# State-space mixer of a hybrid decoder block: y and z kept with channels in rows, norm factors applied at the output product

## The chip, the cores and the metric

The kernel runs on one core of a Trainium2 chip. The metric is the device time of one execution in microseconds; a kernel's time is the median over several runs. All tensors are float32. Where the kernel says "fp32r", a float32 value has been split into a high part and a low part, each held in a reduced form that TensorE takes at its quick rate, and a product is three products: high by high, high by low and low by high.

## The reference

One decoder block for a sequence of 1024 tokens and a width of 1024. A hidden state h feeds two token mixers, whose outputs are merged by gates; a gated conv-FFN follows. Only the first mixer, the state-space one (SSD), and what takes its output is touched here:

```
xbc = silu(causal_dwconv(xbc, conv_w, conv_b))
xs, bm, cm = split(xbc)                 # 16 heads of 64 channels; 2 groups, state 128
dt = softplus(dt_raw + dt_bias); a = -exp(a_log)
# in chunks of 128 tokens; l, s: tokens of a chunk
xd = xs * dt
a_cum = cumsum(dt * a)
decay = exp(where(s <= l, a_cum[l] - a_cum[s], -inf))
cb = einsum('bclgn,bcsgn->bclsg', cc, bc)
y_diag = einsum('bclsgr,bcsgrp->bclgrp', cb[..., None] * decay, xd)
states = einsum('bclgn,bclgrp->bcgrpn', bc, xd * decay_to_end)
prev = running state: prev * chunk_decay + states
y_off = einsum('bclgn,bcgrpn->bclgrp', cc, prev) * exp(a_cum)
y = y_diag + y_off + d_skip * xs
y = y * silu(z)
yg = y in 2 groups of 512 channels
yg = yg * rsqrt(mean(yg * yg) + 1e-5)
y_ssd = yg * norm_w
merged = gate_ssd * (y_ssd @ w_ssd_o) + gate_att * (y_att @ w_attn_o)
```

The norm's factor belongs to a token and a group of 512 channels, so that it can be applied to y, or to the two partial sums (channels 0 to 511, 512 to 1023) of the product with w_ssd_o.

## The kernel before

The kernel is one function with many nested helpers. The order of the instructions on TensorE (PE), VectorE (DVE), ScalarE (ACT) and the sync engine (SP) is fixed by the order in which the code calls them, so an instruction that waits holds back all that stands behind it on its engine. GpSimd (POOL) does a few elementwise steps. SP issues nearly every DMA, in the order of the code; a store that waits for its data holds back the loads behind it. In SBUF, 43 slots of 128 x 1024 float32 are handed out and taken back by name (SL.get, SL.put). In PSUM there are two buffers of two banks (ps_mm), two of one bank (ps_wa) and two single banks (ps_wb, ps_wc).

The stages that matter, in order of time:

*z.* z_mms (L979 to L986) makes z in seven products by four token blocks of 128, with h as the stationary operand and 512 columns of weights moving, so z has tokens in rows (partitions). z_out (L1005) applies silu and stores it to DRAM, one array of 128 tokens by 1024 channels for each chunk.

*The SSD loop* (L1285 to L1334) runs over 16 steps u, chunk c = u // 2 and group g = u % 2, and is filled with the products that make v (fill, which draws 3-product pieces from v_stream), so that TensorE has work while the others prepare. A step's work is spread over helpers:

- chunk_in, for the next step: four transposes bring x, which lies with channels in rows, to tokens in rows (px, in PSUM); ScalarE copies px to xtk; VectorE makes xd = xtk x dt, POOL makes xd times the decay to the end and y = xtk x d_skip; TensorE makes the product of B and C and the transpose of B, and VectorE puts the causal mask on the former.
- chunk_decay and chunk_mask, for the next step: ScalarE makes the decay between tokens, VectorE multiplies it with the masked product of B and C. The result Ms has a 128 x 128 matrix M for each of the group's 8 heads, with the source tokens s in rows.
- chunk_out: po, the product of C with the carried state (128 tokens by 512 channels, not for chunk 0), which VectorE scales by exp(a_cum) into tt; then eight products py with a head's M stationary and 64 columns of xd moving; VectorE adds py to y, POOL adds tt.
- chunk_state: the state that the chunk adds.
- chunk_norm, at every second step: puts a chain of small steps in a queue (later), from which the loop runs one to three at given places (run_bg): y times z on VectorE, squares summed over channels on ScalarE (free with tokens in rows, since the sum runs along the row), the factor, y times the factor on VectorE, the store of y.

The heart of chunk_out:

```
T.matmul(pq, CT[g][:, tok], po[:, g, :], start=True, stop=True)
V.tensor_tensor(v3(tt[:, gs]), v3(pq), bc64(ea[:, c, hs]), op=ALU.mult)
...
T.matmul(py[:, r * 64 : (r + 1) * 64], Ms[u % 3][:, r, :], xd[:, g * GW + r * 64 : g * GW + (r + 1) * 64], start=True, stop=True)
```

*Four blocks of q and k* (n = 0 to 3; w_q, w_k, w_q, w_k), each two halves of 24 products of 512 columns (block_half, which calls mm3). Between the halves stand rope for the block before (ScalarE copies it out of PSUM into qf, VectorE and POOL turn it, split makes a high part thhi on ScalarE and a low part thlo on VectorE), the split of the next block's weights (split_seq), turn_y and the stores of q or k (store_qk: 16 small stores, high and low part in turn). turn_y (L1351 to L1360) brings y, reloaded with tokens in rows by load_y (four arrays yr for 512 tokens at a time), to channels in rows by four transposes in PSUM, from which ScalarE and VectorE make the high and low part, times the norm's weight. Which pieces are turned behind which half is listed in turns.

*Eight blocks of w_ssd_o* (j = 0 to 7), each two halves of 24 products into the two banks of one ps_mm buffer; VectorE then multiplies both halves by one plus the tanh of the gate (mout, L1443) and SP stores them. Between the halves stand, on VectorE, the low part of the next block's weights and, for j = 1 to 4, four differences of w_down pieces that a later stage wants (down_sum, L890), whose loads (down_load) stand on SP behind the k stores.

Attention, the output product and the FFN follow and are not touched.

## Time and profile before

| | before |
|---|---|
| median of 3 runs | 1813.42 us |
| lowest and highest | 1812.23 and 1814.8 us |
| the profiled execution | 1813.67 us |
| its span on the core | 1811.8 us |
| mean granted TensorE clock | 0.999 |
| instructions | 23720 |
| data moved by DMA | 336.22 MB, 133385 packets |

The profile is of one execution, which took 1813.67 us in all, of which 1811.8 lie between its first and last instruction. "Busy" is the time in which an engine executes something; PE is TensorE's products and PEld its loading of stationary operands, which runs beside the products. The granted clock is the share of its full clock that the chip gave TensorE. In a timeline row stand the start in microseconds from the span's start, the duration, the engine, the line, the operation with its output and its inputs, the shapes, how many were put together in the row, and in brackets how long the engine had been idle and what ended that. A row of windows gives a stretch, its length, the busy time and number of instructions of PE, PEld, DVE, ACT and POOL, the granted clock, the share of DMA use and the GB/s. Since TensorE's products are pipelined, a product's duration in such a row is longer than the distance from its start to the next one's.

### The profile page before, as it was taken

Reading aid. Unit: us, or ns where it says so; the run is one execution under the profiler, and the core shown is the slowest. Engines: PE = TensorE matmul, PEld = TensorE weight load, DVE = VectorE, ACT = ScalarE, POOL = GpSimd, SP = SyncE. Lnnn points to the kernel's source line nnn. Section 1 sums busy time; section 2 is a strip of 40 time slices with the busy share of each in tenths; the row PEclk is TensorE's granted clock in tenths of the full one; section 3 lists DMA queues with packets and bytes.
Section 4 is the critical chain, followed back from the end, with each engine's and each line's share of the span. In section 5 each row is a group of like instructions: output and inputs, shape, how many; then the busy total and the mean of one; then the engine's idle time right before and its main releaser. Section 6 shows DMA issues by size and latency. Waiting matters only on the chain.

```text
span 1811.8 us, 23720 instructions
## 1 busy us (share of the span) xinstructions
PE 1788.3 (99%) x8587; PEld 1483.5 (82%) x8587; DVE 1300.5 (72%) x1973; ACT 908.7 (50%) x1758; POOL 148.2 (8%) x156
## 2 busy tenths in 40 slices
PE   7999999999999999999999999999999999999998
PEld 5788888877888888888888888888888888888887
DVE  7887885577664277777666876679898888876545
ACT  8554555665440155565566132655454554564532
POOL 0000000365220000000000103100000000000001
PEclk9999999999999999999999999999999999999999
DMA  9464337465579676656726979313232223378744
GB/s 377 187 204 151 106 105 274 168 209 190 195 187 356 202 198 167 179 153 161 222 77 216 359 248 379 117 55 121 93 133 105 94 101 113 117 240 299 254 153 157
DMA packets 133385, 336.22 MB, mean 186 GB/s; under 512 B 15234, under 2 KB 33554, under 8 KB 133268
## 3 DMA queue, kind: packets, MB, share of 16 engines
q1 hardware_dynamic: 130068, 324.21, 53.7%
q0 software_dynamic: 3200, 10.49, 1.5%
q8 instruction: 68, 1.11, 0.3%
q14 instruction: 49, 0.40, 0.1%
HBM read 239.41 MB, written 95.24 MB: 185 GB/s over the span
## 4 chain that ended last, share of the span: by engine, by line
PE 70%; DVE 4%; ACT 2%; issue 1%; DMA 1%; SPq 0%; POOL 0%; DVEq 0%; POOLq 0%; ACTq 0%
PE upx L1977 4%; PE upx L1978 4%; PE upx L1976 4%; PE o L1626 3%; PE dx L2365 2%; PE dx L2366 2%; PE dx L2364 2%; PE upy L1978 2%; PE upy L1976 2%; PE upy L1977 2%; PE dy L2365 2%; PE dy L2364 2%; PE dy L2366 2%; PE sc L1568 2%; PE ao L118 2%; PE mix L2052 2%
## 5 line engine op out<-in xcount | busy, mean ns | idle before, releaser
L1976 PE MATMUL upx<-t,wu_t 128*128 128x512 f32 x264 | 103.1, 391 | 0.5 <-DVE cv L2429 0.4
L1977 PE MATMUL upx<-t,wu_t 128*128 128x512 f32 x264 | 102.8, 390 | 0.2 <-DVE t L2107 0.2
L1978 PE MATMUL upx<-t,wu_t 128*128 128x512 f32 x264 | 102.8, 389 | 0.0
L1614 ACT COPY aT<-at 128x512 f32<-128x512 f32 (+2 forms) x96 | 46.1, 480 | 112.8 <-PE at L1613 112.8
L1950 ACT ACTIVATE wu_t<-sab 128x512 fp32r<-128x512 f32 x57 | 34.1, 627 | 128.1 <-DVE sab L1967 128.1
L95 DVE TENSOR_TENSOR g_lo<-gst,g_hi 128x1024 fp32r<-128x1024 f32 (+1 forms) x42 | 47.7, 1135 | 50.4 <-ACT g_hi L94 50.2
L1626 PE MATMUL o<-vt,aT 128*128 128x128 f32 x576 | 80.5, 276 | 0.0
L1626 PEld LDWEIGHTS o<-vt,aT 128*128 128x128 f32 x576 | 74.3, 191 | 2.2
L94 ACT ACTIVATE g_hi<-gst 128x1024 fp32r<-128x1024 f32 (+1 forms) x42 | 41.5, 989 | 66.1 <-DMA gst<-gld_s 36.2
L1587 DVE TENSOR_REDUCE nmx<-sc 128x1 f32<-128x640 f32 (+3 forms) x64 | 65.6, 1025 | 2.2
L1567 PE MATMUL sc<-kst,qst 128*128 128x512 f32 (+2 forms) x192 | 64.6, 344 | 0.6 <-ACT p L1589 0.5
L1568 PE MATMUL sc<-klo,qst 128*128 128x512 f32 (+2 forms) x192 | 62.9, 344 | 0.0
L1603 DVE RECIPROCAL rsm<-ssum 128x2 f32<-128x2 f32 x64 | 10.6, 166 | 70.0 <-ACT p L1600 40.0
L1994 DVE SCALAR_TENSOR_TENSOR ug<-cg,vec,ug 128x1023 f32<-128x1023 f32 (+1 forms) x44 | 56.3, 1280 | 6.1 <-ACT ug L1993 5.3
L1976 PEld LDWEIGHTS upx<-t,wu_t 128*128 128x128 f32 x264 | 49.6, 188 | 11.6 <-DVE cv L2429 1.3
L1954 DVE TENSOR_TENSOR wu_t<-sab,wu_t 128x512 fp32r<-128x512 f32 x57 | 39.3, 690 | 26.6 <-ACT wu_t L1950 26.6
L1977 PEld LDWEIGHTS upx<-t,wu_t 128*128 128x128 f32 x264 | 49.6, 188 | 10.7 <-DVE t L2107 0.5
L1978 PEld LDWEIGHTS upx<-t,wu_t 128*128 128x128 f32 x264 | 49.5, 188 | 10.3
L1994 DVE SCALAR_TENSOR_TENSOR uv<-cv,vec,uv 128x1023 f32<-128x1023 f32 (+1 forms) x44 | 56.2, 1277 | 0.9 <-ACT uv L1993 0.9
L2485 POOL TENSOR_TENSOR rsf<-rsf,nhalf 128x1 f32<-128x1 f32 x8 | 5.2, 655 | 623.5 <-DVE rsf L2484 623.5
L1605 DVE SCALAR_TENSOR_TENSOR p<-p,coef,p 128x128 f32<-128x128 f32 (+3 forms) x64 | 52.4, 819 | 2.3
L139 POOL TENSOR_TENSOR sqt<-sqt,nhalf 128x4 f32<-128x4 f32 x16 | 16.5, 1031 | 433.3 <-DVE sqt L138 433.3
(591 smaller groups left out, 5825.0 us busy)
## 6 DMA issues: line engine op xcount, KB each, us to landing
adas<-in_w_ada SPq DMA_DIRECT2D x32, 512.0 KB, 5.6
wuf<-in_w_up SPq DMA_DIRECT2D x22, 512.0 KB, 3.2
gld_s<-gsum SPq DMA_DIRECT2D x22, 512.0 KB, 2.8
gst<-gld_s SPq DMA_DIRECT2D x20, 512.0 KB, 4.5
wdt_raw<-wtd SPq DMA_DIRECT2D x20, 512.0 KB, 4.9
wuv<-in_w_up SPq DMA_DIRECT2D x19, 512.0 KB, 3.3
gld_a<-ug SPq DMA_DIRECT2D x33, 256.0 KB, 2.1
adat<-in_w_ada SPq DMA_DIRECT2D x16, 512.0 KB, 8.4
```

Source lines behind the costliest of these rows:

```text
L1567: T.matmul(sc[:, n0:n1], qs_[s][:, tsl], ks_[s][:, n0:n1], start=True, stop=False)
L1568: T.matmul(sc[:, n0:n1], qs_[s][:, tsl], kl[s][:, n0:n1], start=False, stop=True)
L1587: V.reduce_max(nmx[:, bq, s : s + 1], sc[:, :L], axis=AX.X, negate=True)
L1605: V.scalar_tensor_tensor(pr[0][:, :L], pr[1][:, :L], coef[:, bq : bq + 1], pr[0][:, :L], op0=ALU.mult, op1=ALU.add)
L1626: T.matmul(po_of[j, grp][:, qi, :], at[:, k, :], vt[j % 2][:, kt, :], start=(kt == 0), stop=(kt == i))
L1976: T.matmul(out_, wh, xh_, start=(k == 0 and first), stop=False, skip_group_check=not first)
L1977: T.matmul(out_, wh, xl_, start=False, stop=False, skip_group_check=not first)
L1978: T.matmul(out_, wl, xh_, start=False, stop=(k == end), skip_group_check=not first)
L1994: V.scalar_tensor_tensor(u[:, d:], c_[:, : S - d], fw[:, 2 - d : 3 - d], u[:, d:], op0=ALU.mult, op1=ALU.add)
L2364: T.matmul(o, gh[:, kk, tsl], wh, start=(k == 0 and not more), stop=False, skip_group_check=more)
L2365: T.matmul(o, gh[:, kk, tsl], wl, start=False, stop=False, skip_group_check=more)
L2366: T.matmul(o, gl[:, kk, tsl], wh, start=False, stop=(k == KF - 1), skip_group_check=more)
```

## The change

y and z are kept with channels in rows from the start.

- **z**: in z_mms weights are stationary and h moves, so that z comes out with channels in rows. It is stored in one array, a chunk's 128 tokens being 512 bytes in a row.
- **x**: the ScalarE copy xtk goes. VectorE makes xd from px in PSUM. POOL makes y = x times d_skip from the untransposed x, with d_skip as a column in vec (V_DS). The reload of x for the chunk after the next stands behind that.
- **y products**: xd is stationary now (64 columns, one head), M moves (128 columns). Two heads write to rows 0 to 63 and 64 to 127 of the same 128 columns, so 8 products fill the same bank.
- **Carried state**: four products with 128 columns of the state stationary and C moving, in place of one of 512 columns. exp(a_cum) must now run along the row: chunk_decay makes it with two exponentials of 64 rows each (eb) per step, from the rows of a_cum that are loaded for the decay anyway.
- **Norm**: channels lie across rows, so that the sum over them is made in two stages: VectorE adds up the squares of four 128-channel pieces (reduce_sum, into ssq), and TensorE adds over rows, one product per group with ssq stationary and one column of ones moving (norm_sums). These run in chunk_in two chunks later, for chunk 6 at step 14, and for chunk 7 ahead of the first w_q block. y is stored without its factor.
- **Factors**: behind the first half of the second block the 16 x 128 factors are turned by one transpose, stored (rsd), and reloaded as two rows that are spread over all partitions (rsr).
- **turn_y** becomes split_y, which makes the two parts from the reloaded y, with no transposes.
- **w_ssd_o**: a half block now goes to both banks of a ps_mm buffer, one for each group of channels (so_half); so_out multiplies each by its group's factors, adds them and applies the gate, four VectorE operations for a half block, where before it was one. The result goes into gth in place.

```diff
     def chunk_decay(u):
         c, g = divmod(u, 2)
+        if c > 0:
+            by_two = Ms[u % 3].rearrange("p (j two) t -> p two j t", two=2)
+            for n in range(2):
+                hp = slice(64 * n, 64 * n + 64)
+                A.activation(eb[hp, g], by_two[hp, n], AF.Exp)
...
-                T.matmul(o, xh_, wh, start=(k == 0 and first), stop=False, skip_group_check=not first)
-                T.matmul(o, xh_, wl, start=False, stop=False, skip_group_check=not first)
-                T.matmul(o, xl_, wh, start=False, stop=(k == KH - 1), skip_group_check=not first)
+                T.matmul(o, wh, xh_, start=(k == 0 and first), stop=False, skip_group_check=not first)
+                T.matmul(o, wh, xl_, start=False, stop=False, skip_group_check=not first)
+                T.matmul(o, wl, xh_, start=False, stop=(k == KH - 1), skip_group_check=not first)
...
-            SP.dma_start(zd[4 * half + q][:, c * HALF : (c + 1) * HALF], o)
+            SP.dma_start(zd[:, 4 * half : 4 * half + 4, 4 * c + q, :], o.rearrange("p (c t) -> p c t", t=P))
...
+        if c > 1 and g == 0:
+            norm_sums(pc[:, 2 * P : 2 * P + 2], c - 2)
...
-        A.copy(xtk[:, gs], px)
...
-        V.tensor_tensor(v3(xd[:, gs]), v3(xtk[:, gs]), bc64(dt[:, c, hs]), op=ALU.mult)
+        V.tensor_tensor(v3(xd[:, gs]), v3(px), bc64(dt[:, c, hs]), op=ALU.mult)
...
-        G.tensor_tensor(v3(y[:, gs]), v3(xtk[:, gs]), bc64(rows[:, R_DS + g * RH : R_DS + (g + 1) * RH]), op=ALU.mult)
+        G.tensor_tensor(p4(y[:, gs]), xch[c % 2][:, 4 * g : 4 * g + 4, :], vec[:, V_DS + 4 * g : V_DS + 4 * g + 4, None].broadcast_to([P, 4, P]), op=ALU.mult)
...
-            T.matmul(pq, CT[g][:, tok], po[:, g, :], start=True, stop=True)
-            V.tensor_tensor(v3(tt[:, gs]), v3(pq), bc64(ea[:, c, hs]), op=ALU.mult)
+            for j in range(4):
+                T.matmul(pq[:, j * P : (j + 1) * P], po[:, g, j * P : (j + 1) * P], CT[g][:, tok], start=True, stop=True)
+            V.tensor_tensor(p4(tt[:, gs]), p4(pq), eb[:, g], op=ALU.mult)
         py = ps_wb(f"py{c}_{g}")
         for r in range(RH):
-            T.matmul(py[:, r * 64 : (r + 1) * 64], Ms[u % 3][:, r, :], xd[:, g * GW + r * 64 : g * GW + (r + 1) * 64], start=True, stop=True)
+            T.matmul(py[64 * (r % 2) : 64 * (r % 2) + 64, r // 2 * P : r // 2 * P + P], xd[:, g * GW + r * 64 : g * GW + (r + 1) * 64], Ms[u % 3][:, r, :], start=True, stop=True, skip_group_check=True)
...
         def square():
...
+            SP.dma_start(yd[:, :, c * P : (c + 1) * P], y.rearrange("p (k t) -> p k t", t=P))
+            A.activation(zt, y, AF.Square)
+
+        def sums():
+            V.reduce_sum(ssq, zt.rearrange("p (g j t) -> p g t j", g=2, t=P), axis=AX.X)
             if c < 7:
                 load_z(c + 1)
...
+    def norm_sums(ps, c):
+        need(("y", c))
+        for g in range(2):
+            T.matmul(ps[:, g : g + 1], ssq[:, g, :], ones[:, :1], start=True, stop=True)
+        V.tensor_copy(ssy[:, :, c], ps)
...
-            SP.dma_start(yr[q], yd[4 * half + q])
+            SP.dma_start(yr[q], yd[:, 2 * q : 2 * q + 2, half * HALF : (half + 1) * HALF])
...
+            if u == 14:
+                norm_sums(ps_wc("norms6")[:, :2], 6)
...
-        for q in range(4):
-            T.transpose(ps[:, q * P : (q + 1) * P], yr[q][:, k * P : (k + 1) * P], ident)
...
+    def split_y(k, half):
+        t = yT[k][half] = new_hl(f"yT{k}_{half}")
+        nw, src = vec[:, V_SN + k : V_SN + k + 1], yr[k // 2][:, k % 2, :]
+        A.activation(t[:, 0, :], src, AF.Copy, scale=nw)
+        V.scalar_tensor_tensor(t[:, 1, :], src, nw, t[:, 0, :].bitcast(F32), op0=ALU.mult, op1=ALU.subtract)
...
+        pn = ps_wc("norms")
+        norm_sums(pn[:, :2], 7)
+        SL.put(sm2)
+        for g in range(2):
+            rstd_of(ssy[:, g], ssy[:, g], 1.0 / GW, 1e-5)
         for n in range(4):
...
                 if n == 1 and half == 0:
                     load_y(1)
+                    pn = ps_wb("normT")
+                    T.transpose(pn[:16, :P], ssy.rearrange("p g c -> p (g c)"), ident)
+                    V.tensor_copy(f(dtc)[:16, :], pn[:16, :P])
+                    SP.dma_start(rsd, f(dtc)[:16, :])
...
+        rsr = [SL.get(f"rsr{g}") for g in range(2)]
+        for g in range(2):
+            SP.dma_start(rsr[g], rsd[8 * g : 8 * g + 8].rearrange("c t -> (c t)")[None].broadcast_to([P, S]))
+
+        def so_half(j, half):
+            ps = ps_mm(f"so{j}_{half}")
+            for g in range(2):
+                mm3(ps[:, g, :], [((seq_w[j + 4][0][:, k, :], seq_w[j + 4][1][:, k, :]), (yT[k][half][:, 0, :], yT[k][half][:, 1, :])) for k in range(4 * g, 4 * g + 4)])
+            return ps
+
+        def so_out(ps, gth, half):
+            hsl = slice(half * HALF, (half + 1) * HALF)
+            for g in range(2):
+                V.tensor_tensor(sev[:, g, :], ps[:, g, :], rsr[g][:, hsl], op=ALU.mult)
+            V.tensor_tensor(sev[:, 0, :], sev[:, 0, :], sev[:, 1, :], op=ALU.add)
+            V.scalar_tensor_tensor(gth[:, hsl], gth[:, hsl], 1.0, sev[:, 0, :], op0=ALU.add, op1=ALU.mult)
...
-            block_half(ps[:, 1, :], seq_w[j + 4], yT, 1)
-            for half in range(2):
-                hsl = slice(half * HALF, (half + 1) * HALF)
-                V.scalar_tensor_tensor(mout[:, hsl], gth[:, hsl], 1.0, ps[:, half, :], op0=ALU.add, op1=ALU.mult)
+            so_out(ps, gth, 0)
+            so_out(so_half(j, 1), gth, 1)
```

Three places show how the order of the engines moves; in each, the first block is the order before and the second the order with the change, with the line, the operation, output and inputs, and the shape.

TensorE at the end of the SSD loop: py is the last y product, v_7 the last piece of the v products that fill the loop, and w_qp the first block of w_q.

```order
L1221 MATMUL py_1_3919<-xd,M_2452 128x64 x8
L1152 MATMUL v_7_3892<-wv_3_hi,hT_1_264 128x512
L1153 MATMUL v_7_3892<-wv_3_lo,hT_1_264 128x512
L1154 MATMUL v_7_3892<-wv_3_hi,hT_1_264 128x512
L1152 MATMUL v_7_3892<-wv_3_hi,hT_1_266 128x512
L1153 MATMUL v_7_3892<-wv_3_lo,hT_1_266 128x512
L1154 MATMUL v_7_3892<-wv_3_hi,hT_1_266 128x512
L116 MATMUL w_qp_3967<-hT_0_78,w_q_hi 128x512
L117 MATMUL w_qp_3967<-hT_0_78,w_q_hi 128x512
```

```order
L1227 MATMUL po_1_3947<-xbcT_2177,prev_2694 128x128 x4
L1231 MATMUL py_1_3953<-M_2438,xd 64x128 x8
L1160 MATMUL v_7_3922<-wv_3_hi,hT_1_264 128x512
L1161 MATMUL v_7_3922<-wv_3_lo,hT_1_264 128x512
L1162 MATMUL v_7_3922<-wv_3_hi,hT_1_264 128x512
L1160 MATMUL v_7_3922<-wv_3_hi,hT_1_266 128x512
L1161 MATMUL v_7_3922<-wv_3_lo,hT_1_266 128x512
L1162 MATMUL v_7_3922<-wv_3_hi,hT_1_266 128x512
L1275 MATMUL norms<-ones,sm_1136 128x1 x2
L117 MATMUL w_qp_4005<-hT_0_78,w_q_hi 128x512
```

The y products come in another shape, the product with the carried state in four pieces, and two one-column sums (norms) stand between the last v product and the first product of w_q; they read what the norm's chain makes of the last chunk (sm holds ssq).

The sync engine, from the last store of v to the first stores of q: yd is y in DRAM, yr its reload, thhi and thlo the parts of the turned q, rsd the factors.

```order
L1168 DMA vd_597<-vev 128x512
L1255 DMA yd_605<-yt_2704 128x1024
L1271 DMA yr_3667<-yd_602 128x1024
L1271 DMA yr_3668<-yd_603 128x1024
L1271 DMA yr_3669<-yd_604 128x1024
L1271 DMA yr_3670<-yd_605 128x1024
L455 DMA qd_653<-thhi 16x1024
L456 DMA qd_653<-thlo 16x1024
```

```order
L1176 DMA vd_591<-vev 128x512
L1255 DMA yd<-yt_2690 1024x1x128
L1280 DMA yr_3687<-yd 128x2x512
L1280 DMA yr_3688<-yd 128x2x512
L1280 DMA yr_3689<-yd 128x2x512
L1280 DMA yr_3690<-yd 128x2x512
L1417 DMA rsd<-dtc 16x128
L457 DMA qd_640<-thhi 16x1024
L458 DMA qd_640<-thlo 16x1024
```

The reload stands where it stood, in another shape and from the one array; the store of the factors is new, between the reload and the first store of q.

VectorE in the first two w_ssd_o blocks: so is the product in PSUM, mout or gth what is stored, wdr the w_down pieces, w_ssd_o_lo the low part of the next block's weights.

```order
L95 TENSOR_TENSOR w_ssd_o_lo<-w_ssd_o_raw,w_ssd_o_hi 128x1024
L1443 SCALAR_TENSOR_TENSOR mout_4391<-gth_4389,so_4397 128x512 x2
L95 TENSOR_TENSOR w_ssd_o_lo<-w_ssd_o_raw,w_ssd_o_hi 128x1024
L890 TENSOR_TENSOR wdr_4445<-wdr_4445 128x512
L890 TENSOR_TENSOR wdr_4445<-wdr_4446,wdr_4445 128x512
L890 TENSOR_TENSOR wdr_4446<-wdr_4446,wdr_4445 128x512
L890 TENSOR_TENSOR wdr_4446<-wdr_4446 128x512
L1443 SCALAR_TENSOR_TENSOR mout_4392<-gth_4390,so_4487 128x512 x2
```

```order
L1435 TENSOR_TENSOR sev<-so_1_4426,rsr_4351 128x512
L1435 TENSOR_TENSOR sev<-so_1_4426,rsr_4352 128x512
L1436 TENSOR_TENSOR sev<-sev 128x512
L1437 SCALAR_TENSOR_TENSOR gth_4355<-gth_4355,sev 128x512
L96 TENSOR_TENSOR w_ssd_o_lo<-w_ssd_o_raw,w_ssd_o_hi 128x1024
L891 TENSOR_TENSOR wdr_4410<-wdr_4410 128x512
L891 TENSOR_TENSOR wdr_4410<-wdr_4411,wdr_4410 128x512
L891 TENSOR_TENSOR wdr_4411<-wdr_4411,wdr_4410 128x512
L891 TENSOR_TENSOR wdr_4411<-wdr_4411 128x512
L1435 TENSOR_TENSOR sev<-so_0_4459,rsr_4351 128x512
L1435 TENSOR_TENSOR sev<-so_0_4459,rsr_4352 128x512
```

The second block begins with the second half of block 0, the row before it (not shown) being the same four operations for its first half. Each half block is now emptied by four operations, where before one row of two emptied both; the first half of block 1 is emptied behind the four differences, ahead of its second half.

85 lines of the change are left out of this document (34 added, 51 removed).

## The prediction

> **What bounds the kernel now.** I read the busy line of the page first, then the chain of waits, then a table by stretches for the stages that the change touches, then the waits of TensorE's weight loads.
>
> ```profile
> PE 1788.3 (99%) x8587; PEld 1483.5 (82%) x8587; DVE 1300.5 (72%) x1973; ACT 908.7 (50%) x1758; POOL 148.2 (8%) x156
> ...
> PE 70%; DVE 4%; ACT 2%; issue 1%; DMA 1%; SPq 0%; POOL 0%; DVEq 0%; POOLq 0%; ACTq 0%
> ...
> 325.00:490.00 165.00, 164.67 (x864) 132.00 (x863) 113.44 (x159) 95.30 (x244) 78.62 (x64) 1.00 0.56 196
> 490.00:575.00 85.00, 84.92 (x402) 70.54 (x401) 50.65 (x61) 24.10 (x30) 13.64 (x4) 1.00 0.75 229
> ...
> PEld so L118 <- DVE w_ssd_o_lo L95: 0.5, 1, 0.5
> ```
>
> TensorE has work in 164.67 of 165 us of the SSD stage and in 84.92 of 85 us behind it; the only wait near the w_ssd_o blocks is one of 0.5 us. So each microsecond of TensorE's own work that goes in these stages shortens the program, and each new wait of TensorE lengthens it. VectorE (113 of 165 us) and ScalarE (95) set nothing as long as they stay just ahead. That is the whole question here: the change takes matmul time away and puts dependences in its place.
>
> **What TensorE saves.** Three bursts of the timeline price it.
>
> ```profile
> 489.58 1.47 PE L1357 MATMUL ytr<-ident,yr 128*128 128x128 f32 x12
> ...
> 491.12 0.40 PE L117 MATMUL w_kp<-hT,w_k_hi 128*128 128x512 f32 x1
> ...
> 360.01 1.02 PE L1217 MATMUL po<-prev,xbcT 128*128 128x512 f32 x2
> 360.87 1.89 PE L1221 MATMUL py<-xd,M 128*128 128x64 f32 x16
> ...
> 362.88 0.39 PE L1153 MATMUL v<-wv_lo,b 128*128 128x512 f32 x1
> ...
> 78.23 0.39 PE L118 MATMUL gs<-hT,wgs_lo 128*128 128x512 f32 x1
> 78.55 3.64 PE L745 MATMUL dt<-hr,dtw 128*32 128x512 f32 x32
> ...
> 82.46 0.40 PE L117 MATMUL gs<-hT,wgs_hi 128*128 128x512 f32 x1
> ```
>
> Starts matter here, not durations: in a steady block a 512-column product starts every 0.23 us (476.63 to 477.79 in a later fence, five of them). The row behind a burst is the second product of the next block, so the burst ended 0.23 us ahead of it.
>
> *The y transposes.* Twelve take 491.12 - 0.23 - 489.58 = 1.31 us, 0.109 each. All 64 go: **-7.0 us**.
>
> *The y products.* One burst (8 heads, 16 passes) takes 362.88 - 0.23 - 360.87 = 1.78 us, 0.11 per pass, though it moves only 64 columns: the load of 128 stationary columns sets the pace. Now 64 columns are stationary and 128 move. A float32 pass of 512 columns takes (360.87 - 360.01)/2 = 0.43, so one of 128 takes 0.107 to 0.11. Whether two heads run side by side shows in the dt product, which already writes four column groups: 32 passes of 0.43 would take 13.8 one by one; it takes from 78.46 (78.23 + 0.23) to 82.23, 3.77 us. That is 8 times 0.43 and 0.33 for getting into the grouped layout and out of it. So a new burst costs 8 x 0.11 + 0.33 = 1.21, saving 0.57; sixteen save **-9.1 us**. Bounds: no overlap, 16 x 0.11 + 0.33 = 2.09, +5.0 in all; no cost of changing layout, 0.88, -14.4. I take the dt row, which is the same mechanism with four groups for two.
>
> The Trainium skill ("TensorE: Matmul & The Clock Gate", Part 3) gives 2.38 times for three column groups, not three. By that share two groups would run 1.6 times as fast, a burst would take 1.44, the saving would be 5.5 us, and the sum below would be 1819.7. The dt row of this trace, 4.0 times for four groups, disagrees, and the trace decides.
>
> **What TensorE gains.** The carried-state product is cut in four 128-column pieces: 8 passes of 0.11 for two of 0.43, +0.04 in 14 places, **+0.5 us**. The sums over channels add 16 one-column products: 32 passes, each held by the load of 128 columns at 0.11, +3.5, and about 0.3 for the transpose of the factors and for two sums that stand alone: **+3.8 us** (between 1 if a one-column pass needs no full load and 4.5). The z products and the w_ssd_o products keep number and size; only what is stationary or where a sum is split changes: 0.
>
> So TensorE's own work falls by 11.8 us. ScalarE loses the copies of x and gains two exponentials per step, VectorE loses the scaling and gains one reduction per chunk; both have a third of the stage idle, so I cost that at nothing (28 exponentials of about 0.63, as the 512-wide ScalarE row below, are 18 us and eight reductions of 1.2 are 10 us if that cover is gone). More and smaller packets for z and y lie under 0.56 of DMA use; nothing waits for them within two steps.
>
> **New wait 1: the last chunk's norm sum.** It stands in TensorE's queue between the last v product and the first w_q block, and needs y of chunk 7 finished, times z, squared and summed.
>
> ```profile
> 476.63 0.39 PE L1153 MATMUL v<-wv_lo,hT 128*128 128x512 f32 x1
> ...
> 477.79 0.39 PE L116 MATMUL w_qp<-hT,w_q_hi 128*128 128x512 f32 x1
> ...
> 476.54 0.69 DVE L1223 TENSOR_TENSOR yt<-py,yt 128x512 f32<-128x512 f32 x1 [1.03 <-PE py L1221]
> 477.38 1.29 POOL L1227 TENSOR_TENSOR yt<-yt,tt 128x512 f32<-128x512 f32 x1 [6.12 <-DVE yt L1223]
> 478.70 1.23 DVE L1259 TENSOR_TENSOR yt<-yt,zt 128x1024 f32<-128x1024 f32 x1 [1.47 <-POOL yt L1227]
> 480.01 0.63 ACT L1247 ACTIVATE zt<-yt 128x512 f32<-128x512 f32 x1 [1.44 <-DVE yt L1259]
> ...
> L1587 DVE TENSOR_REDUCE nmx<-sc 128x1 f32<-128x1024 f32 x16 | 19.6, 1225 | 0.5
> ```
>
> Today nothing on TensorE waits for this chain, and w_q starts at 477.79. In the changed order the square starts at 480.01, takes 1.06 (a 1024-wide ScalarE row, below), the reduction 1.23 and two handovers 0.15: 482.45. Leaving the grouped layout puts TensorE 0.15 later, at 477.94. Wait: **+4.5 us**. Behind it stand the whole w_q block and all that follows. The sums of the other chunks are asked for a full step later and cost nothing.
>
> **New wait 2: the store queue behind rope.** SP's order is what changed. The reload of y (second half) and the store of the turned factors stand ahead of the 16 q stores. The reload now waits for the y splits of ScalarE and VectorE, no longer for TensorE's transposes; the factor store waits for a VectorE copy behind those splits.
>
> ```profile
> 477.99 0.59 ACT L1167 COPY vev<-v 128x512 f32<-128x512 f32 x1 [4.33 <-PE v L1154]
> ...
> 491.94 1.03 ACT L1378 ACTIVATE qf<-w_qp 128x1024 f32<-128x1024 f32 x1
> 499.13 1.06 ACT L94 ACTIVATE thhi<-qf 128x1024 fp32r<-128x1024 f32 x1 [6.16 <-DVE qf L1382]
> ...
> 501.36 1.22 DVE L95 TENSOR_TENSOR w_q_lo<-w_q_raw,w_q_hi 128x1024 fp32r<-128x1024 f32 x1
> 502.50 2.06 DVE L1360 SCALAR_TENSOR_TENSOR yT<-ytr,vec,yT 128x512 fp32r<-128x512 f32 x3
> ...
> 497.56 1.75 SPq L1271 DMA_DIRECT2D yr<-yd  x4
> 500.21 0.32 SPq L455 DMA_DIRECT2D qd<-thhi  x1
> ...
> 508.57 0.42 SPq L456 DMA_DIRECT2D qd<-thlo  x1
> 509.03 0.42 SPq L455 DMA_DIRECT2D qd<-thhi  x1
> ...
> 511.11 1.06 ACT L94 ACTIVATE thhi<-qf 128x1024 fp32r<-128x1024 f32 x1 [6.70 <-DMA qd<-thhi]
> ```
>
> I count from the end of the first w_q block, 489.58 today. ScalarE can take the result 0.2 later (477.79 to 477.99); today it comes to it at 491.94. From its start the rope and low-part chain takes 12.6 to the end of the third y split (504.56). So the copy is done at 13.0 and the q stores start at 13.4, where today they start at 10.6 and would now be ready at 8.5. They follow each other by 0.46; the last store of the high part is issued at 13.4 + 14 x 0.46 = 19.9, and the next rope may overwrite it 2.1 later (509.03 to 511.11), at 22.0. Behind that rewrite on ScalarE and VectorE stand the parts of the second w_k block: high part at 24.0, low part (two VectorE operations of 1.2) at 25.5. Without transposes the block is due at 22.0 (two blocks of 48 products, 10.9 each, and one turn). It can start at about 25.0: **+3.0 us**.
>
> What is late next: four y splits stand ahead of each following rope on ScalarE, 2.4 us. The third rope starts at 26.4, and its chain of 10.6 (491.94 to 502.58) with 0.6 of VectorE's own splits brings the first w_ssd_o low part at 37.6; the block, due at 36.0, needs it with its third product: **+1.2 us**. The fourth rope starts at 38.5, the next low part is done at 49.8.
>
> **New wait 3: fewer banks.** A half block now fills a pair of banks, so a bank must be emptied within one half block, 5.5 us, where today it had a block. Each half takes four VectorE operations for one.
>
> ```profile
> 539.98 1.28 DVE L1443 SCALAR_TENSOR_TENSOR mout<-gth,so 128x512 f32<-128x512 f32 x2
> ...
> 537.69 0.32 SPq L458 DMA_DIRECT2D khd<-thhi  x1
> ...
> 546.70 1.79 SPq L885 DMA_DIRECT2D wdr<-in_w_down  x4
> ...
> 553.75 0.69 DVE L890 TENSOR_TENSOR wdr<-wdr 128x512 f32<-128x512 f32 x1
> ```
>
> In VectorE's order the first emptying stands behind that low part: 49.8 + 1.28 = 51.1, block 1 is due at 48.1: +3.0, where today 0.5 is lost: **+2.5 us**. The emptying of block 1 stands behind the four w_down differences, whose loads stand behind the k stores: 9.0 from the first store to the loads and 7.7 to the last difference. Stores from 47.5 put it at 64.2, the bank free at 65.5; block 2 is due at 62.0: 3.5, or 2.6 if the stores pack better; I take **+3.0 us**. From block 3 on I find a microsecond or more to spare, with four operations, 2.7 us of VectorE, per 5.5.
>
> **The sum**, on the profiled execution (1811.8 span, 1813.67 in all, 0.25 above the median of 1813.42): -7.0 - 9.1 + 0.5 + 3.8 + 4.5 + 3.0 + 1.2 + 2.5 + 3.0 = +2.4, so **1816 us**: the saving is spent on waits.
>
> **The rivals.** *The clock falls in wait 1 (slower).* TensorE stands idle for 4.5 us, longer than anywhere in today's program behind the first microseconds.
>
> ```profile
> 14.85 1.22 PE L257 MATMUL xbc<-hT,wf_hi 128*128 128x512 f32 x2 [1.94 <-ACT hT L227]
> ...
> 19.29 1.05 PE L257 MATMUL gs<-hT,wf_hi 128*128 128x512 f32 x2
> 20.14 1.16 PE L216 MATMUL xbc<-hr,ones 128*128 128x512 f32 x2
> ...
> 1805.12 0.39 PE L2366 MATMUL dx<-wdt_hi,g_lo 128*128 128x512 f32 x1
> ...
> 1805.00:1811.00 6.00, 0.51 (x3) 0.08 (x1) 2.32 (x5) 0.69 (x2) 0.54 (x1) 0.83 0.47 175
> ```
>
> After the last matmul the granted clock averages 0.83 over 6 us: half speed for the last 2, so it fell some 3.7 us after it. At the start two products took 0.85 (19.29 to 20.14), half speed, 5.3 us after dense work began. 5.3 us at half speed lose 2.6: 1818.7. It decides where the wait passes the point at which the clock falls, which is near 4.5. The Trainium skill (same page, Part 1) has a free-running window of 3.4 us, which would hit an idle 4.5 one time in three and need at least 3.4 us to release; the trace's 3.7 agrees, with one case.
>
> *Store and bank waits are shorter (not slower).* If the q stores are out by 10.6 as today, wait 2 goes (4.2 us), and the fourth rope starts a microsecond earlier: about 5.5 less, 1810.5. For it: each step rests on a margin of about a microsecond. Against: the order on SP is fixed.
>
> *No overlap of column groups* (the change doesn't do what it says): 14.1 more, 1830. Against it stands the dt row.
>
> *VectorE falls behind in the w_ssd_o blocks or the SSD loop*: one further wait like the 3.0 in two or three blocks, 1823; VectorE's 50.65 of 85 us plus some 33 for the emptying is close (16 halves, three more operations of 0.69 each).
>
> **Chances.** Forecast 0.45 (own range 1812 to 1820), clock 0.18, shorter waits 0.19, no overlap 0.07, VectorE 0.11. Range 1805 to 1828: the low end is the shorter waits with the layout change free, the high end short of no overlap. 0.2%, about what a measurement can tell, is 3.6 us: slower (above 1817) 0.48, all of clock, VectorE and no overlap and 0.12 of the forecast; within 0.38, which is 0.28 of the forecast and 0.10 of the shorter waits; faster (below 1810) the remaining 0.14.
>
> **What would show it.** y products that start in pairs 0.01 apart, a burst of 1.2; TensorE idle about 4.5 before the first w_q block, released by the reduction; q stores starting behind the factor store; idle of some 3, 1, 3 and 3 us before the second w_k block and the first three w_ssd_o blocks. Wrong would be bursts near 2 us, or blocks that follow each other without gaps.

## The result, and the profile after

The changed kernel takes 1828.51 us (median of 4 runs, 1827.87 to 1828.95), the kernel before 1813.88 in the same comparison (4 runs): a ratio of 1.0081, with a 95% interval of 1.0064 to 1.0099. It is slower, by about 14.6 us. Forecast were 1816 with a range of 1805 to 1828: the sign was that of the forecast, the size was not, and the time lies half a microsecond outside the range.

The profiled execution spans 1826.5 us, 14.7 more than before. The page's busy line and the chain of waits of the changed kernel:

```profile
PE 1786.0 (98%) x8640; PEld 1478.9 (81%) x8640; DVE 1323.9 (72%) x2016; ACT 917.0 (50%) x1745; POOL 143.3 (8%) x150
...
PE 84%; DVE 7%; ACT 3%; DMA 2%; issue 2%; POOL 1%; SPq 1%; DVEq 0%; POOLq 0%; ACTq 0%
```

TensorE is busy 2.3 us less, in a span 14.7 us longer. Where it stands idle from the SSD loop to the w_ssd_o blocks is in the list of its waits (line, releaser, microseconds in total, times, the longest):

```profile
PE norms L1275 <- DVE sm L1259: 6.4, 2, 5.0
PE so L117 <- DVE sev L1435: 5.8, 2, 4.1
PE w_kp L117 <- ACT w_k_hi L95: 3.8, 1, 3.8
PE px L1275 <- DVE sm L1259: 1.0, 1, 1.0
PE v L1161 <- DVE wv_lo L932: 0.5, 1, 0.5
PE w_kp L119 <- DVE w_k_lo L96: 0.2, 1, 0.2
```

That is 17.7 us, where TensorE of the kernel before is without work for 0.4 (0.33 and 0.08) by the two windows that the prediction shows of these stages. The waits are longer than the whole loss, so other terms of both signs must stand beside them. The timeline has the four long waits at these rows:

```profile
482.20 0.98 PE L1275 MATMUL norms<-ones,sm 128*128 128x1 f32 x4 [5.00 <-DVE sm L1259]
...
522.16 0.79 PE L117 MATMUL w_kp<-hT,w_k_hi 128*128 128x512 f32 x1 [3.83 <-ACT w_k_hi L95]
...
549.24 0.47 PE L117 MATMUL so<-yT,w_ssd_o_hi 128*128 128x512 f32 x1 [1.67 <-DVE sev L1435]
...
564.48 0.76 PE L117 MATMUL so<-yT,w_ssd_o_hi 128*128 128x512 f32 x1 [4.08 <-DVE sev L1435]
```

and a table of windows, laid where the clock record changes, shows what follows them (stretch, length, busy time and number of instructions of PE, PEld, DVE, ACT, POOL, then the granted clock, the DMA share and GB/s):

```profile
477.50:480.91 3.41, 0.00 (x0) 0.00 (x0) 1.97 (x2) 2.25 (x3) 0.28 (x1) 1.00 0.93 320
480.91:487.74 6.83, 5.54 (x15) 4.61 (x16) 5.63 (x10) 1.33 (x2) 4.08 (x2) 0.50 0.31 84
518.46:521.87 3.41, 0.00 (x0) 0.00 (x0) 0.68 (x1) 1.76 (x2) 0.00 (x0) 1.00 0.77 211
521.87:528.70 6.83, 6.31 (x14) 4.57 (x15) 6.80 (x9) 3.60 (x6) 1.17 (x1) 0.50 0.68 122
559.42:562.83 3.41, 0.98 (x5) 0.48 (x3) 2.41 (x4) 0.00 (x0) 0.00 (x0) 1.00 0.96 273
562.83:569.66 6.83, 5.18 (x12) 4.13 (x13) 6.51 (x10) 1.06 (x1) 0.00 (x0) 0.50 0.82 291
```

In each of the waits of 5.0, 3.8 and 4.1 us the granted clock falls to 0.50 and stays there for 6.83 us. TensorE is busy for 5.54, 6.31 and 5.18 us of these stretches. Products of 512 columns start 0.427 apart there (484.04, 484.47, 484.89 in the timeline) and 0.227 apart at full clock, so that 47% of that busy time is lost: 2.6, 3.0 and 2.4, together 8.0 us. (The expectations below reckon with half of the time from the end of each wait: 2.8, 3.3 and 2.6, together 8.6. That is 0.6 too much.)

The balance is drawn from the first v product to the first product of attention, 292.1 us before (323.89 to 616.00) and 307.8 after (324.47 to 632.29): 15.7 more. The waits behind the loop make 14.8 of it (5.0, 3.8 and 0.2, 1.7, 4.1), half clock 8.0, the small waits in the loop 2.8 (1.0 and 0.5, and the other 1.4 of norms) less the 0.4 of before. What is left, -9.5, is put down to TensorE's own work, forecast at -11.8; it is a difference and was not measured as such, and experiment 8 finds about 2 us more of hold-ups in the loop that this list does not show. The stages behind, which the change does not touch, happen to be 1.4 us shorter in this profile than in that of the kernel before (1187.7 from 632.29 to the last product at 1819.95, for 1189.1 from 616.00 to 1805.12), and what lies ahead of the loop is 0.6 longer: together about the 14.7 of the spans.

### The profile page after: what moved, and what is told of

Same layout as the page of the kernel before. It is cut to its first block, busy times and chain, and to the rows that moved or that the text cites. A ratio compares the mean times of both kernels' runs of the same rounds, so it can differ in the third digit from the quotient of the medians.

```text
span 1826.5 us, 23848 instructions
## 1 busy us (share of the span) xinstructions
PE 1786.0 (98%) x8640; PEld 1478.9 (81%) x8640; DVE 1323.9 (72%) x2016; ACT 917.0 (50%) x1745; POOL 143.3 (8%) x150
## 4 chain that ended last, share of the span: by engine, by line
PE 84%; DVE 7%; ACT 3%; DMA 2%; issue 2%; POOL 1%; SPq 1%; DVEq 0%; POOLq 0%; ACTq 0%
PE upx L2001 4%; PE upx L2000 4%; PE upx L2002 4%; PE o L1650 3%; PE dx L2388 2%; PE dx L2390 2%; PE dx L2389 2%; PE upy L2001 2%; PE upy L2000 2%; PE upy L2002 2%; PE sc L1592 2%; PE dy L2388 2%; PE dy L2390 2%; PE dy L2389 2%; PE sc L1591 2%
## 5 line engine op out<-in xcount | busy, mean ns | idle before, releaser
L1627 DVE RECIPROCAL rsm<-ssum 128x2 f32<-128x2 f32 x64 | 10.6, 166 | 70.1 <-ACT p L1624 40.0
L2000 PEld LDWEIGHTS upx<-t,wu_t 128*128 128x128 f32 x264 | 49.6, 188 | 12.1 <-DVE cv L2453 1.8
L2001 PEld LDWEIGHTS upx<-t,wu_t 128*128 128x128 f32 x264 | 49.6, 188 | 10.6 <-DVE t L2131 0.5
L117 PE MATMUL so<-yT,w_ssd_o_hi 128*128 128x512 f32 x128 | 51.0, 398 | 5.8 <-DVE sev L1435 5.8
```

What stands on the lines that cost most here:

```text
L2000: T.matmul(out_, wh, xh_, start=(k == 0 and first), stop=False, skip_group_check=not first)
L2001: T.matmul(out_, wh, xl_, start=False, stop=False, skip_group_check=not first)
```

## The experiments

Two pairs of theories were tested. Theory A: the clock falls because TensorE stands idle, so that each long wait costs its length and some 3 us more. Theory B: it falls by the new forms of products, or at its own time. The second pair came from the blocks of q and k. Theory C: the second wait comes from the order of the stores on SP. Theory D: the chain of rope, weight parts and y parts takes longer for a block than TensorE without transposes, so that it sets the pace and a wait that is removed comes back further on. In the kernel before, a block with its share of the y transposes takes 12.7 us of TensorE ((528.44 - 477.79) / 4), and ScalarE's copies of q or k keep up with it (491.94, 503.38, 516.76 and 529.44, 12.5 apart in the mean). A block of 48 products alone takes 10.9. What the chain takes when TensorE does not pace it is seen in experiment 6.

Times are set against the 1828.51 of the changed kernel. The kernel before, which ran beside each experiment, came to between 1813.2 and 1814.6, so nothing is read from a difference of less than about 1 us.

**1. TensorE kept busy in its waits.**

```diff
+        def idle_mms(name, n, w):
+            ps = ps_wb(name)
+            for i in range(n):
+                T.matmul(ps, w[0][:, 0, :], hT[0][0][:, 0, :], start=(i == 0), stop=(i == n - 1))
+
+        idle_mms("idle1", 20, seq_w[0])
         pn = ps_wc("norms")
         norm_sums(pn[:, :2], 7)
...
+            if n == 3:
+                idle_mms("idle2", 15, seq_w[2])
...
+            if j == 2:
+                idle_mms("idle3", 16, seq_w[5])
```

> The changed kernel with TensorE kept busy in its three long waits: 20, 15 and 16 useless 512-column products (0.23 us each) into a spare bank ahead of the last chunk's norm sum, the second w_k block and w_ssd_o block 2. Nothing that the waits wait for is changed. Theory A (the clock falls because TensorE stands idle): no record of half clock behind the waits, and what follows them is 2.8, 3.3 and 2.6 us shorter; if nothing else sets the pace, 1828.5 - 8.6 = 1819.9. Where ScalarE's and VectorE's chain behind rope sets the pace after the second wait, the 3.3 comes back as a wait before the first w_ssd_o blocks, and the time is about 1823. Theory B (the clock falls because of the new forms of products, or whenever): the half-clock stretches stay, 1828.5.

1825.97 us, 2.5 less. None of the three half-clock stretches is there any more. Windows over the first two places, and over a new one:

```profile
477.50:484.30 6.80, 6.30 (x30) 4.95 (x29) 4.94 (x7) 3.52 (x5) 1.40 (x1) 1.00 0.62 215
518.93:525.80 6.87, 5.93 (x25) 4.61 (x26) 6.76 (x9) 3.54 (x6) 1.26 (x1) 1.00 0.68 131
542.82:546.24 3.42, 0.68 (x3) 0.23 (x3) 3.38 (x5) 0.65 (x1) 0.00 (x0) 1.00 1.02 368
546.24:549.65 3.41, 3.40 (x8) 2.73 (x9) 3.24 (x5) 1.06 (x1) 0.00 (x0) 0.50 0.76 268
```

Theory A holds and B falls: the same new products, the same waits for data, and full clock. But of the 8.0 us of half clock only 2.5 come off. Part of this is the experiment's own doing: in the third place the useless products run on when the bank has long been emptied (560.66, the end of the second row), so that they hold TensorE some 1.7 us too long.

```profile
558.83 3.79 PE L1395 MATMUL idle<-hT,w_ssd_o_hi 128*128 128x512 f32 x16
559.38 1.28 DVE L1443 TENSOR_TENSOR sev<-so,rsr 128x512 f32<-128x512 f32 x2
```

Another part has moved: the first w_ssd_o blocks now wait 0.7 and 2.8 us (0 and 1.7 in the changed kernel), where the slower clock had hidden it, and the latter wait makes the clock fall again, for 3.41 us. That is theory D's sign; 1823, which its expectation named, was not reached.

**2. Heads of a burst not in pairs.**

```diff
-        for r in range(RH):
+        for r in (0, 2, 4, 6, 1, 3, 5, 7):
             T.matmul(py[64 * (r % 2) : 64 * (r % 2) + 64, ...
```

> The changed kernel with the y products of a burst in the order of heads 0, 2, 4, 6, 1, 3, 5, 7, so that neighbours write the same 64 rows and none run side by side. If the shorter burst comes from two heads side by side, it grows from 1.1 to about 16 x 0.107 + 0.33 = 2.04 us, and the time by some 13 to 15 us, to 1841 to 1843 (a little of it hidden where the loop waits today). If it comes from the smaller stationary operand (64 columns loaded for 128), the burst stays near 1.1 and the time at 1828.5.

1833.69 us, 5.2 more: between the two expectations. A burst of the changed kernel, with the product of the carried state ahead of it and two v products behind, and one of this kernel:

```profile
360.59 1.05 PE L1227 MATMUL po<-xbcT,prev 128*128 128x128 f32 x8
361.57 1.09 PE L1231 MATMUL py<-M,xd 128*64 128x128 f32 x16
362.59 0.50 PE L1160 MATMUL v<-wv_hi,b 128*128 128x512 f32 x1
362.93 0.39 PE L1161 MATMUL v<-wv_lo,b 128*128 128x512 f32 x1
```

```profile
341.61 1.58 PE L1231 MATMUL py<-M,xd 128*64 128x128 f32 x16
343.12 0.50 PE L1160 MATMUL v<-wv_hi,hT 128*128 128x512 f32 x1
```

From its start to the next product a burst takes 1.02 in pairs (362.59 - 361.57) and 1.51 so (343.12 - 341.61), 0.49 more; sixteen make 7.8, of which the loop's small waits hide 1.8 (they fall from 2.8 to 1.0 here), which leaves 6.0 for the 5.2 measured. The stationary operand is as small in both kernels, so it is the pairs that run side by side, and it is worth at least 0.49 a burst. The order tried does not take all of it away: in the trace the single products start 0.109 apart at the beginning and at the end of the burst, but the eight in its middle 0.055 apart in the mean, so the last of the first four heads and the first of the second four seem to run beside each other.

**3. The last norm sum later.**

```diff
-        pn = ps_wc("norms")
-        norm_sums(pn[:, :2], 7)
...
         for n in range(4):
...
                 block_half(ps[:, half, :], seq_w[n], hT, half)
+                if (n, half) == (0, 0):
+                    pn = ps_wc("norms")
+                    norm_sums(pn[:, :2], 7)
...
```

> The changed kernel with the last chunk's norm sum and its factors behind the first half of the first w_q block, 5.5 us later on TensorE and behind nothing else that is new on VectorE. Theory A: the wait of 5.0 goes, and the half clock behind it (2.8). TensorE is then 7.8 us earlier at the end of that block; VectorE, busy with the y parts and the adaLN sums, can follow by about 5.9, so about 2 come back in the next wait: 1822 to 1823. Theory B: only the 5.0, or less, with half clock at the same place or another: 1824 to 1826.

1823.63 us, 4.9 less, which lies between the ranges of the two theories; the clock decides for A. The wait and its half clock are gone, and those behind have grown: 0.7 before a third product, 4.3 and 0.7 at the second w_k block, 1.2 and 4.5 at the w_ssd_o blocks. The half clock still follows the 4.3 and the 4.5.

**4. The q stores first.**

```diff
                 if n == 1 and half == 0:
-                    load_y(1)
...
-                    SP.dma_start(rsd, f(dtc)[:16, :])
                 if half == 0 and old is not None:
                     store_qk(*old[:2], hi, lo)
+                if n == 1 and half == 0:
+                    load_y(1)
+                    SP.dma_start(rsd, f(dtc)[:16, :])
```

> The changed kernel with SP's order of before for one thing: the second reload of y and the store of the factors stand behind the 16 q stores. Theory C (the store order makes the second wait): the wait of 3.8 before the second w_k block falls to about 0.4 and the half clock behind it (3.3) goes, 1828.5 - 6.7 = 1822 or less. Theory D (the chain of rope, weight parts and y parts on ScalarE and VectorE takes 12.2 us for a block and TensorE without transposes 10.9, so that it sets the pace whatever the stores do): that wait goes too, but the chain moves forward by 4.6 only, and waits of 1 to 4 stand before the first three w_ssd_o blocks: 1824, not below 1823.

1823.48 us, 5.0 less. The wait before the second w_k block is gone altogether, so its place in the store queue was rightly named; but these stand in its stead:

```profile
530.16 0.50 PE L117 MATMUL so<-yT,w_ssd_o_hi 128*128 128x512 f32 x1 [0.95 <-ACT w_ssd_o_hi L95]
531.61 0.50 PE L119 MATMUL so<-yT,w_ssd_o_lo 128*128 128x512 f32 x1 [0.72 <-DVE w_ssd_o_lo L96]
545.04 0.77 PE L117 MATMUL so<-yT,w_ssd_o_hi 128*128 128x512 f32 x1 [2.71 <-DVE sev L1436]
561.01 0.47 PE L117 MATMUL so<-yT,w_ssd_o_hi 128*128 128x512 f32 x1 [3.32 <-DVE sev L1436]
```

7.7 us of waits for the 9.8 that the changed kernel has from there on (3.8, 0.2, 1.7 and 4.1): theory D, in its number too (1824 was expected, not below 1823).

**5. The bank emptied first.**

```diff
+            so_out(ps, gth, 0)
             if 1 <= j <= KSO:
                 for n in range(4):
                     down_sum(wdr[(j - 1) % 2], j - 1, n, SP)
-            so_out(ps, gth, 0)
```

> The changed kernel with one thing exchanged in VectorE's order: the emptying of a block's first half stands ahead of the four w_down differences. If the third wait (4.1 before w_ssd_o block 2) comes from the emptying behind differences that wait for their loads, it goes with the half clock behind it (2.6): 1828.5 - 6.7 = 1822. If VectorE has too much to do in these blocks in any order, the wait moves by half a block and the time stays within 2 of 1828.5.

1823.10 us, 5.4 less. The wait of 4.1 and the half clock behind it are gone; 0.5 stands before block 3 instead. The third wait was the emptying behind the differences.

**6. The three moves together.**

> The changed kernel with the norm sum later, the q stores first and the banks emptied first, all three. If each wait has a cause of its own, all go with their half clock: 1828.5 - 14.6 - 8.6 = 1805. Theory D (the chain of rope, weight parts and y parts, 12.2 us for a block against TensorE's 10.9, sets the pace): the two earlier moves have brought the end of the wait before block 1 forward by 6.7 and 4.2, to about 538.3; 11.2 us of products follow to where the third wait ended: about 17 us less, 1811 to 1814, with waits of 1 to 4 before the first w_ssd_o blocks.

1812.95 us; against the kernel before 0.9995 (0.9985 to 1.0004), no difference. Theory D's number, not 1805. The profiled execution has full clock throughout, and the waits of the chain:

```profile
501.02 0.50 PE L119 MATMUL w_qp<-hT,w_q_lo 128*128 128x512 f32 x1 [0.71 <-DVE w_q_lo L96]
512.68 0.50 PE L119 MATMUL w_kp<-hT,w_k_lo 128*128 128x512 f32 x1 [0.45 <-DVE w_k_lo L96]
523.79 0.50 PE L117 MATMUL so<-yT,w_ssd_o_hi 128*128 128x512 f32 x1 [0.35 <-ACT w_ssd_o_hi L95]
525.24 0.50 PE L119 MATMUL so<-yT,w_ssd_o_lo 128*128 128x512 f32 x1 [0.71 <-DVE w_ssd_o_lo L96]
539.13 0.47 PE L117 MATMUL so<-yT,w_ssd_o_hi 128*128 128x512 f32 x1 [3.17 <-DVE sev L1437]
```

Every block is late by a little, and what releases it is the weights' part that follows rope or, last, the emptying that stands behind the fourth rope. Here the chain's own period shows, in ScalarE's high parts of q and k:

```profile
509.17 1.06 ACT L95 ACTIVATE thhi<-qf 128x1024 fp32r<-128x1024 f32 x1 [6.90 <-DVE qf L1385]
521.73 1.06 ACT L95 ACTIVATE thhi<-qf 128x1024 fp32r<-128x1024 f32 x1 [7.18 <-DMA khd<-thhi]
533.87 1.06 ACT L95 ACTIVATE thhi<-qf 128x1024 fp32r<-128x1024 f32 x1 [6.77 <-DVE qf L1385]
```

They are 12.6 and 12.1 us apart, the former held by stores of k, against TensorE's 10.9.

**7. Rope in two pieces.** With the three moves, and the other work put in the gap in which VectorE waits for POOL:

```diff
     def rope(kind, b, ps):
...
         V.tensor_tensor(sw, sw, rops, op=ALU.mult)
+
+    def rope_end():
         V.tensor_tensor(qf, qf, sw, op=ALU.add)
         split(hi, lo, qf)
...
                 for k in turns[n][half]:
                     split_y(k, n // 2)
+                if half == 0 and old is not None:
+                    rope_end()
```

> The kernel with the three moves, and rope in two pieces: the weight parts and the y parts stand, on ScalarE and VectorE, in the gap in which POOL turns q or k, ahead of the last addition and the high and low part. Nothing is done less. Theory D: the chain for a block falls from 12.2 to about 9 us, below TensorE's 10.9, and the waits before the w_k, w_q and first w_ssd_o blocks go: 1804 to 1806. If something else sets the pace there (VectorE's load, the k stores, the loads), the waits stay: 1811 or more.

1821.04 us, 8 more than the three moves, where 7 to 9 less were expected. In the timeline:

```profile
492.86 3.43 POOL L1383 TENSOR_TENSOR qf<-qf,ropc 128x1024 f32<-128x1024 f32 x1 [4.11 <-DVE sw L1382]
493.96 3.42 DVE L96 TENSOR_TENSOR w_q_lo<-w_q_raw,w_q_hi 128x1024 fp32r<-128x1024 f32 x1
...
513.51 1.34 ACT L1362 ACTIVATE yT<-yr,vec 128x512 fp32r<-128x512 f32 x2 [8.59 <-DMA yr<-yd]
...
515.60 1.22 DVE L1387 TENSOR_TENSOR qf<-qf,sw 128x1024 f32<-128x1024 f32 x1
```

The low part of the weights, 1.22 us elsewhere, takes 3.42 while POOL's product of two tensors runs: the gap of VectorE was no free time. And in the third block the y parts, which I had put ahead of rope's end, wait for the reload of y (8.6 us), and the addition behind them with it. Waits of 4.4 and 5.8 us in the w_ssd_o blocks follow, with half clock.

**8. The same, with the norm sums one step later.**

```diff
-        if c > 1 and g == 0:
+        if c > 1 and g == 1:
             norm_sums(pc[:, 2 * P : 2 * P + 2], c - 2)
...
-            if u == 14:
+            if u == 15:
                 norm_sums(ps_wc("norms6")[:, :2], 6)
```

> The kernel before, and the norm sums of chunks 0 to 6 one step later in the SSD loop, at the second group's turn and at step 15. If the waits of 0.9, 0.5 and 1.4 us in the loop come from VectorE's reduction (1.9 us) being just behind, they go: 2 to 3 us less than the kernel with rope in two pieces, 1802. If the reduction of the next chunk now waits for the sum, VectorE falls behind and it is no faster.

"The kernel before" is here that of experiment 7. 1816.26 us, 4.8 less than that kernel, where 2 to 3 were expected. No wait of TensorE over 0.2 us is left in the loop: the 2.6 of the three named are gone (1.0, 0.5 and 1.1 in the seventh kernel), and from the first v product to the second block it takes 4.6 us less (159.6 for 164.2), so that about 2 more came from hold-ups which the list of waits does not show. The sums had been asked for too early.

**9. Rope's product on VectorE,** in one piece again, with the three moves:

```diff
-        G.tensor_tensor(qf, qf, ropc, op=ALU.mult)
+        V.tensor_tensor(qf, qf, ropc, op=ALU.mult)
```

> The kernel with the three moves, and the product of q or k with the cosines on VectorE (1.2 us) where POOL took 3.44; the order is otherwise that of the three moves, rope is in one piece. The kernel with rope in two pieces showed a low part of weights at 3.42 us for 1.22 while POOL's product ran, so the gap in the chain was no free time of VectorE. Theory D (the chain of 12.2 us for a block sets the pace): it falls by 1.2 for each of four blocks, and of the 5.0 us of waits in the blocks 4 to 5 go: 1808 to 1809. If VectorE, now with about 9.7 us of work for a block of 10.9, sets the pace itself, there is no gain: 1812 to 1813.

1811.30 us, 1.65 less than the three moves; 4 to 5 were expected. Against the kernel before, which was 0.7 faster beside this run than beside that one, the ratio is 0.9993 (0.9984 to 1.0002) for 0.9995, so a gain over the three moves is not shown. 4.4 us of waits remain in the blocks, and in this profile the clock falls behind two of them, by very little:

```profile
522.09:525.50 3.41, 1.47 (x5) 0.95 (x6) 3.15 (x4) 3.41 (x6) 0.00 (x0) 1.00 0.55 139
525.50:528.92 3.42, 3.42 (x9) 2.67 (x9) 3.39 (x6) 1.12 (x2) 0.00 (x0) 0.50 0.65 120
```

Its eleven times lie at 1810.1 to 1812.2 (eight) and 1813.6 to 1814.9 (three, the profiled one among them), which fits a clock that falls at the same waits in some executions and not in others; one profile cannot show it. ScalarE's list of waits names what sets the pace of the last two ropes now: thhi waits 8.0 and 5.9 us for stores of k and q to end, not for VectorE.

**10. All moves.** The three, rope's product on VectorE, the sums later, and the weights' parts ahead of the parts of q and k:

```diff
         V.tensor_tensor(qf, qf, sw, op=ALU.add)
-        split(hi, lo, qf)
...
                     split_seq(n + 1)
+                    if old is not None:
+                        split(hi, lo, qf)
```

> The kernel before, the norm sums one step later, and the weights' high part on ScalarE ahead of the high part of q or k, the weights' low part on VectorE ahead of the low part of q or k (in none of POOL's time now). No waits in the blocks beyond 0.5, no waits in the loop: the three moves' 5.7 and the loop's 2.6 go, 1812.95 - 8.3 = 1804 to 1806, which would be 0.5% faster than the kernel before the change: TensorE's own work less 11 us, with two handovers left. If it is VectorE, 1809 or more.

("The kernel before" in this expectation is that of experiment 9.) 1807.06 us, between the two expectations; against the kernel before the change 0.9967 (0.9955 to 0.9979): faster than that and than the changed kernel. One long wait is left, with half clock behind it, and ScalarE shows where the chain now hangs:

```profile
533.55 0.77 PE L117 MATMUL so<-yT,w_ssd_o_hi 128*128 128x512 f32 x1 [5.36 <-DVE sev L1438]
```

```profile
503.31 1.06 ACT L95 ACTIVATE thhi<-qf 128x1024 fp32r<-128x1024 f32 x1 [5.75 <-DMA qd<-thhi]
...
516.29 1.06 ACT L95 ACTIVATE thhi<-qf 128x1024 fp32r<-128x1024 f32 x1 [4.20 <-DMA khd<-thhi]
...
528.13 1.06 ACT L95 ACTIVATE thhi<-qf 128x1024 fp32r<-128x1024 f32 x1 [6.47 <-DMA qd<-thhi]
```

The high part can be written again only when the 16 stores of the block before are out; from one to the next are 13.0 and 11.8 us, still above TensorE's 10.9. With the weights' parts ahead of it, that delay no longer holds the next block, but at the end it holds the first emptying, which stands behind the last low part (done at 530.44) and then waits another 0.98 and 0.60 us for the two loads of the factors.

**11. The factors earlier, and the first emptying ahead of that low part.**

```diff
+                if n == 3 and half == 0:
+                    SL.put(*yr[:2])
+                    rsr = [SL.get(f"rsr{g}") for g in range(2)]
+                    for g in range(2):
+                        SP.dma_start(rsr[g], ...
                 if half == 0 and old is not None:
                     store_qk(*old[:2], hi, lo)
...
                 split_seq(j + 5)
+                so_out(ps, gth, 0)
                 split(hi, lo, qf)
```

> The kernel with all moves, and two more: the load of the factors stands ahead of the third block's 16 stores on SP (in slots that the first half of the reloaded y gives back), and the first emptying in the w_ssd_o blocks stands on VectorE ahead of the last low part of k. The one wait left there, 5.4 us before w_ssd_o block 1 with 1.8 lost to half clock behind it, came from the emptying behind that low part and behind the factors, whose load was issued behind the q stores. If so, it falls to about 0.5: 1807.06 - 6.7, about 1800. If the emptying waits for something else (the gate's load), a wait of 2 to 5 stays: 1803 or more.

1807.97 us, 0.9966 (0.9954 to 0.9979): no gain over all moves, where about 7 were expected if the wait fell; the expectation's other case, a wait for the gate's load, came out. The wait named fell from 5.4 to 1.5. In the trace the emptying's last operation waits for the gate's load, so the last low part comes 2.7 us later (531.88 for 529.22). The loads of w_down, which stand on SP behind the last stores of k, are issued no earlier for it: at 540.16, for 540.84 with all moves, in an execution whose last v product came 0.7 us sooner too (471.54 for 472.25). The first difference waits 4.0 us for them, and the second half of block 2, which TensorE now reaches earlier, waits 3.4 us for a bank that is emptied behind the differences, with half clock:

```profile
528.94 0.47 PE L117 MATMUL so<-yT,w_ssd_o_hi 128*128 128x512 f32 x1 [1.46 <-DVE sev L1439]
548.90 0.65 PE L117 MATMUL so<-yT,w_ssd_o_hi 128*128 128x512 f32 x1 [3.37 <-DVE sev L1439]
```

**12. A control: rope's moves in the kernel before.**

> A control: the kernel before the change with the same two moves in its rope (the product with the cosines on VectorE, the weights' parts ahead of the high and low part of q or k). If the chain on ScalarE and VectorE sets the pace only where the y transposes are gone, nothing changes here, since TensorE already has no waits: 1813 to 1814. If these moves are worth something by themselves, it is faster, and part of what the moves brought the changed kernel is no merit of the change.

1813.31 us, 0.9997 (0.9988 to 1.0006): nothing, as expected. Rope's chain costs time only where the transposes are gone, and what its moves bring is the change's own saving, let through. (The other moves change orders that only the changed kernel has.)

## Why the prediction was wrong

**TensorE's own work** was right in each large term. The y transposes: the four blocks of q and k took 50.65 us with them, and 192 products at 0.227 are 43.6: about 7.0, as forecast. A y burst by the prediction's measure (362.93 - 0.23 - 361.57) takes 1.13, forecast 1.21; the dt row was a good stand-in. The product in four pieces takes 0.98 (361.57 - 360.59) for 0.86, +1.7 in 14 places where +0.5 was put. A chunk's two sums take 0.37 where they need not wait (375.67 to 376.04), 3.0 for eight chunks, forecast 3.5. Added up, with the 0.3 for the transpose of the factors as forecast, this is -12.4 (the bursts -10.4), where the balance gives about -11.5 with the hold-ups of experiment 8.

**The waits** were right in place and, as a sum, in size: forecast 4.5, 3.0, 1.2, 2.5 and 3.0 (14.2), measured 5.0, 3.8 and 0.2, 0, 1.7 and 4.1 (14.8). Two differences have their rows. The reduction, over a strided view and with 256 results in a row for one, takes 1.9 us, not the 1.23 of the row that it was costed by:

```profile
480.17 1.89 DVE L1259 TENSOR_REDUCE sm<-zt 128x256 f32<-128x1024 f32 x1 [1.12 <-ACT zt L1256]
```

And the wait of 1.2 before the first w_ssd_o block is not there, since half clock made the block ahead of it longer; at full clock 0.7 of it appears (experiment 1).

**The step that failed** is the one on the clock, in the rivals: "It decides where the wait passes the point at which the clock falls, which is near 4.5". The sum itself has no term for the clock. There is no such point in the length of one wait, and the step was asked only of the first wait. In every profile here the changes of the clock lie whole multiples of 3.413 us apart: in the changed kernel it falls at 480.91, 521.87 and 562.83, which are 12 steps apart each. It falls at the end of a step in which TensorE was idle for 57% or more (1.94 us of 3.41 in the ninth kernel, 2.43 in the third wait here). It stayed up at 56% (1.92, from 1805.50 in the ninth kernel) and, one step ahead of a fall in the seventh, at 51% (1.73):

```profile
520.36:523.77 3.41, 1.68 (x8) 0.99 (x6) 3.38 (x5) 2.09 (x3) 1.89 (x1) 1.00 0.75 138
523.77:527.18 3.41, 0.79 (x3) 0.67 (x4) 3.41 (x3) 0.00 (x0) 1.49 (x1) 1.00 0.74 137
527.18:530.60 3.42, 3.42 (x10) 2.64 (x9) 2.30 (x3) 1.77 (x3) 0.00 (x0) 0.50 0.55 156
```

Any wait of 3.9 us has 1.95 in one step, wherever the step begins; waits of 2 to 3.9 depend on the grid. By their measured lengths the waits of 5.0 and 4.1 were thus certain to cost the clock, and that of 3.8 nearly so. By the lengths that were forecast (4.5, 3.0 and 3.0) only the first was, and the other two falls depended on the grid. Three falls at 2.6, 3.0 and 2.4, one of which a rival had priced (2.6), make 8.0 of the 12.3 us by which the sum was short; the loop's small waits and hold-ups make most of the rest. The trace of before held the hint: its clock fell 3.7 us after the last product, less than the 4.5 of wait 1. The Trainium skill ("TensorE: Matmul & The Clock Gate", Part 1) has a free-running window of 3.4 us, and the grid agrees; its state table asks for a whole idle window, and there the measurement differs: 57% was enough. The same page of the Trainium skill ("Why this matters for your kernels") warns of idle gaps over about 3 us; by that line all three waits count, as they did.

**A second, smaller step:** "The sums of the other chunks are asked for a full step later and cost nothing." They make 2.4 of the loop's 2.8 us of waits (1.0 and 1.4), as the reduction ends just behind TensorE's request; a step later nothing waits for them, and 4.6 us come off (experiment 8).

**The rivals.** The clock rival, given 0.18 and 1818.7, was the true mechanism, at three places instead of one. No overlap and a VectorE that falls behind did not come. "If the q stores are out by 10.6" was tested by experiment 4: the wait goes, and of the 9.8 us of waits from there on 7.7 are left in other places, since the chain's period is above TensorE's. The prediction did carry the delay on from rope to rope (26.4, 38.5), but that rival priced an earlier store as if all behind it came forward too; the transposes had been the chain's cover.
